# Tying the gain scalings and the splits of the K, Q and gate weights behind the first matmul of the projection before

## The chip, the cores and the metric

The kernel runs on one core of one Trainium2 chip. The metric is the device time of one execution in microseconds; lower is better. Before the change it is 2731.74 us (the median of three runs, 2731.46 to 2737.39).

## What is computed

A two-layer encoder trunk over 2048 frames of width 1024, in float32. Layer A is a gated MLP, layer B is chunked attention with a relative-position bias whose keys and values come from the output of layer A. Cut to what matters here:

```
h  = rms_norm(x, a_norm_g);  u, v, z = split(h @ w_in, 3)
x  = x + (gelu(u) * (W_s LayerNorm(gelu(v)) + b) * silu(z)) @ w_out      # layer A
k, v = split(rms_norm(x, kv_norm_g) @ w_kv, 2)                           # shared K and V
q, z = split(rms_norm(x, b_norm_g) @ w_qz, 2)
o  = softmax(q k^T / 8 + bias, own chunk and the 8 chunks before) v      # 16 heads of 64
x  = x + (o * silu(z)) @ w_b_out
out = rms_norm(x, final_norm_g)
```

## The kernel before

**Arithmetic.** Every float32 matrix product is made of three matmuls on operands that are split into a high and a low part (`mm3`, lines 112 to 115: high by high, high by low, low by high). A split is one cast on ScalarE (ACT) that makes the high part and one subtraction on VectorE (DVE) that makes the low part.

**Stages.** Layer A comes first, then the V projection for the four sequence tiles of 512 frames, then stage B: the attention and the output product. This stage starts with the first projection matmul at 1549.0 us and reaches the end of the program.

**Stage B.** The outer loop runs over the four tiles t, the inner one over the eight pairs p of heads. A pair needs three projections: Q (c = 1), K (c = 0) and the gate z (c = 2). Each is one call of `one` (lines 1214 to 1223): it fetches a 128 x 1024 block of weights with `weights` (lines 189 to 200), takes one PSUM bank, and makes 8 x 3 = 24 matmuls into it. So there are 96 projections, 24 to each tile. While a pair's scores, softmax, transposes and value products run, the projections of the next pair, and a part of the output product of the tile before, are mixed in between, some matmuls at a time (`ahead`, lines 1581 to 1600).

**A projection's weights.** In the first tile (t = 0) `weights` loads the block from the input (line 196), GpSimd (POOL) multiplies it by the norm's gain (`scaled`, lines 170 to 173), a DMA stores the scaled block for later tiles (line 198), and `split_in` (lines 185 to 187) casts it into `wh` on ACT and subtracts it into `wl` on DVE. In the later tiles the scaled block is loaded (line 194) and only split. The raw block has four buffers in the first tile, which are shared with the activations' tiles, and two of its own later. `wh` and `wl` come from a pool of eight buffers (`w_tile`), which the output product's weights use too: four projections can be prepared ahead, where nothing else holds the pool.

**What sets the order.** The program is written out flat. The framework decides at build time, by its own estimate of times, in which order each engine's instructions are queued; at run time each engine takes its queue in order, with semaphores where there is a dependency of data or buffers. All DMAs of this kernel are issued from the SP queue, in order too. An extra edge between two instructions, without a semaphore (`add_manual_dep` with the class NoSync), tells this ordering that one instruction comes after another. Layer A already uses such edges in a helper:

```python
def paced(ins):
    if "evict" in last:
        behind(ins, last["evict"])
```

It ties, for example, the POOL product of `merge_u` (line 756) behind the latest DVE eviction.

**The end of the V stage.** The V projection of the last tile takes its left operands from splits `Shv` and `Slv` (lines 269 and 270); its evictions are DVE subtractions (line 1136), ACT casts (line 1135) and POOL additions (line 1159).

Of the kernel before, what the change touches and what calls it, by code (L numbers as in the profile page):

```python
# [13 lines left out]
ALU = mybir.AluOpType  # L14
# [3 lines left out]
P = 128  # L18
S = 2048
D = 1024  # L20
KD = D // P
# [12 lines left out]
def trunk_kernel(  # L34
# [19 lines left out]
    nc = tc.nc  # L54
# [32 lines left out]
    kg = cst.tile([P, KD, 1], F32, name="kg")  # L87
    bg = cst.tile([P, KD, 1], F32, name="bg")
# [21 lines left out]
    mm, tpose = nc.tensor.matmul, nc.tensor.transpose  # L110

    def mm3(ps, lh, ll, rh, rl, first, last):
        mm(ps, lh, rh, start=first, stop=False)  # L113
        mm(ps, lh, rl, start=False, stop=False)  # L114
        mm(ps, ll, rh, start=False, stop=last)  # L115

    xT = {}
    xf = {}
# [41 lines left out]
    def reload(t):  # L160
        th, tl = x_tiles(t)
        for b in range(TB):
# [4 lines left out]
            nc.scalar.copy(oh, x3)  # L167
            tv(tl[:, :, b * P : (b + 1) * P], x3, oh.bitcast(F32), op=sub)

    def scaled(raw, gain):  # L170
        k = gain.shape[1]
        r3 = raw[:].rearrange("p (k c) -> p k c", k=k)
        nc.gpsimd.tensor_tensor(r3, r3, gain.broadcast_to([P, k, 1024 // k]), op=ALU.mult)

    def w_tile(name):
        return sh.tile([P, 1024], F32R, tag="T", name=name, bufs=8)
# [3 lines left out]
    def raw_w(t, name):  # L180
        if t:
            return raws[0].tile([P, 1024], F32, tag="wr", name=name, bufs=2)
        return sh.tile([P, 1024], F32, tag="raw", name=name, bufs=4)

    def split_in(raw, wh, wl):
        nc.scalar.copy(wh[:], raw[:])  # L186
        tv(wl[:], raw[:], wh[:].bitcast(F32), op=sub)  # L187

    def weights(t, p, c):
        name = f"b{t}_{p}_{c}"  # L190
        raw = raw_w(t, f"raw_{name}")
        w = w_tile(f"wh_{name}"), w_tile(f"wl_{name}")
        if t:
            nc.sync.dma_start(raw[:], wk3[p][c][:])
        else:
            nc.sync.dma_start(raw[:], w_kqz[p, :, c, :])
            scaled(raw, (bg if c else kg)[:, :, :])
            nc.sync.dma_start(wk3[p][c][:], raw[:])
        split_in(raw, *w)
        return w  # L200

    def o_right(t):
# [19 lines left out]
    def v_early(q, ph):  # L222
        if q == 0:
            tag = "hh" if ph == 1 else "hl"
            big = sh.tile([P, 4, 1024], F32R, tag=tag, name=f"vw_{ph}")
            for i in range(2):
                vw[ph, i] = (big[:, 2 * i, :], big[:, 2 * i + 1, :])
        raw = sh.tile([P, 1024], F32, tag="raw", name=f"rv_{ph}_{q}", bufs=4)
        nc.sync.dma_start(raw[:], vwf[ph, q][:])
        return lambda: split_in(raw, *vw[ph, q])  # L230
# [3 lines left out]
    def strassen(name, right, left, evict, look):  # L234

        todo = [(ph, jp) for ph in PHS for jp in range(2)]
        rts, views = {}, {}

        def weigh(n):
            for ph in PHS[:n]:  # L240
                if ph not in rts:
                    rts[ph] = right(ph)

        def ready(i):
            if i < len(todo):
                views[i] = left(*todo[i])

        weigh(1)
        ready(0)
        for i, (ph, jp) in enumerate(todo):  # L250
            ps = pmm.tile([P, 512], F32, tag="mm", name=f"{name}_{ph}_{jp}")
            vs = views.pop(i)
            for k in range(4):
                hi, lo = rts[ph][k // 2]
                c = slice((k % 2) * 512, (k % 2) * 512 + 512)
                mm3(ps[:], *vs[k], hi[:, c], lo[:, c], k == 0, k == 3)
                if k == 1:
                    weigh(i // 2 + (2 if jp else 1 + look))
                    ready(i + 1)
                if k < 3:  # L260
                    yield
            evict(ph, jp, ps[:])
            yield
# [46 lines left out]
    with ExitStack() as actx:  # L310
# [169 lines left out]
        def product(ps, s, t):  # L480

            nk = len(s)
            for k in range(nk):
                hi, lo = t[k // 2]
                c = slice((k % 2) * 512, (k % 2) * 512 + 512)
                mm3(ps[:], s[k][0], s[k][1], hi[:, c], lo[:, c], k == 0, k == nk - 1)
# [248 lines left out]
        def mix(n, r, q, part):  # L735
            vh, vl = mixp[n, r, q]
            ws = wsp[n]
            if part == 0:
                mt[n, r, q] = up[0].tile([P, 2, 512], F32, tag="m", name=f"m{n}_{r}_{q}", bufs=4)
            m = mt[n, r, q]  # L740
            px = up[1].tile([P, 2, 2, P], F32, tag="mx", name=f"mx{n}_{r}_{q}_{part}", bufs=2)
            hs = [2 * part, 2 * part + 1]
            cs = [slice(h * P, h * P + P) for h in hs]
            for i, (h, c) in enumerate(zip(hs, cs)):
                mm3(
                    px[:, i], ws[:, 0, h, :], ws[:, 1, h, :], vh[:, :, c], vl[:, :, c], True, True
                )
            for i, (h, c) in enumerate(zip(hs, cs)):
                hh = (n - 2) * 4 + h
                nc.scalar.activation(  # L750
                    m[:, :, c], px[:, i], AF.Identity, scale=0.5, bias=bsh[:, hh : hh + 1]
                )
# [50 lines left out]
        start = {}  # L803
# [387 lines left out]
    with ExitStack() as bctx:  # L1191
# [22 lines left out]
        def one(t, p, c):  # L1214
            wh, wl = weights(t, p, c)
            acc = pmm.tile([P, T], F32, tag="mm", name=f"pj{t}_{p}_{c}")
            for k in range(KD):
                hh, hl = xT[t][k]
                sl = slice(k * P, (k + 1) * P)
                mm3(acc[:], wh[:, sl], wl[:, sl], hh, hl, k == 0, k == KD - 1)  # L1220
                if k < KD - 1:
                    yield None
            yield acc

        def project(t, p):
            for acc in one(t, p, 1):
                yield
            for hd in range(2):
                qh = sb.tile([P, T], F32R, tag="Q", name=f"Qh{t}_{p}_{hd}", bufs=8)
                ql = sb.tile([P, T], F32R, tag="Q", name=f"Ql{t}_{p}_{hd}", bufs=8)  # L1230
                r, r2 = halves(hd)
                nc.scalar.mul(qh[r, :], acc[r, :], 0.125)
                nc.vector.scalar_tensor_tensor(
                    ql[r, :], acc[r, :], 0.125, qh[r, :].bitcast(F32),
                    op0=ALU.mult, op1=ALU.subtract,
                )
                for x_ in (qh, ql):
                    nc.sync.dma_start(x_[r2, :].bitcast(F32), x_[r, :].bitcast(F32))
                qt[t, p, hd] = (qh, ql)
            for acc in one(t, p, 0):  # L1240
                yield
            for hd in range(2):
                r, r2 = halves(hd)
                kx = sb.tile([P, 2 * T], F32R, tag="K", name=f"K{t}_{p}_{hd}", bufs=4)
                nc.scalar.copy(kx[r, T:], acc[r, :])
                nc.vector.tensor_tensor(
                    kx[r2, T:], acc[r, :], kx[r, T:].bitcast(F32), op=ALU.subtract
                )
                if t + 1 < NT:
                    nc.sync.dma_start(khd[t][p][hd], kx[:, T:].bitcast(F32))  # L1250
                if t > 0:
                    nc.sync.dma_start(kx[:, :T].bitcast(F32), khd[t - 1][p][hd])
                kt[t, p, hd] = kx
# [7 lines left out]
        def gate(t, p):  # L1261
            for acc in one(t, p, 2):
                yield
            z = sb.tile([P, T], F32, tag="Z", name=f"Z{t}_{p}", bufs=2)
            nc.scalar.activation(z[:], acc[:], AF.Tanh, scale=0.5)
            nc.vector.scalar_tensor_tensor(
                z[:], z[:], 1.0, acc[:], op0=ALU.add, op1=ALU.mult
            )
            zt[t, p] = z
# [311 lines left out]
        def ahead(t, p):  # L1581

            if p + 1 < NPAIR:
                yield from project(t, p + 1)
                values(t, p + 1)
                if p == 0:
                    yield from gate(t, 0)
                yield from gate(t, p + 1)
                if t:
                    yield from some(outs[t - 1], SHARE[t][p])  # L1590
            else:
                if t + 1 < NT:
                    reload(t + 1)
                if t:
                    yield from some(outs[t - 1], 4)
                if t + 1 < NT:
                    yield from project(t + 1, 0)
                    values(t + 1, 0)
                if t:
                    yield from some(outs[t - 1], 8)  # L1600
# [9 lines left out]
        first = ahead(0, 0)  # L1610
# [103 lines left out]
```

## Time and profile before

| | before |
|---|---|
| median of 3 runs | 2731.74 us |
| profiled execution, its own time | 2731.49 us |
| profiled execution, span of its instructions | 2729.7 us |
| mean granted TensorE clock | 0.987 |
| TensorE (PE) busy | 2629.2 us, 96% |
| VectorE (DVE) busy | 1970.0 us, 72% |
| ScalarE (ACT) busy | 1327.0 us, 49% |
| GpSimd (POOL) busy | 907.7 us, 33% |

The profile is of one execution, which took 2731.49 us, 1.79 us of them outside the span and 0.25 us under the median. PE's bar is high throughout, so the time that can be won or lost is in the single stretches where it waits, and in the stretches in which its clock is granted at half. In a row of the timeline stand the start, the length, the engine, the source line, the operation with its output and inputs, how many were merged, and in brackets the idle time before it with what ended it. A row of the waits has the waiter and the one waited for, then the total in us, the number of times, and the longest.

### The profile page before, as it was taken

What the parts mean: (1) busy time and instruction counts of PE and PEld (TensorE: products, weight loads), DVE (VectorE), ACT (ScalarE), POOL (GpSimd) and SP (SyncE); (2) the same over time, 40 slices, a digit from 0 to 9 for tenths busy, and PEclk for the clock granted to TensorE, in tenths of its full rate; (3) what the DMA queues carried; (4) which work ended last, traced back from release to release, by engine and by line L of the source; (5) the groups of instructions that cost most, each with busy time, mean ns of one, the idle gap of its engine ahead of it and who ended that gap; (6) DMA issues with size and microseconds to landing.
All of it is one profiled execution on the core that took longest, in us unless ns stands there. A gap on an engine that the chain in (4) does not pass through costs nothing. (4 is left out here: it accounts for less than half of the span.)

```text
span 2729.7 us, 38869 instructions
## 1 busy us (share of the span) xinstructions
PE 2629.2 (96%) x13216; PEld 2199.6 (81%) x13216; DVE 1970.0 (72%) x3097; ACT 1327.0 (49%) x2360; POOL 907.7 (33%) x906
## 2 busy tenths in 40 slices
PE   8999999999999999999989899899999999999997
PEld 7788888888888888888867677788887888788875
DVE  5655676676666668667677777777778778877787
ACT  5422242433434345332455455656656566656553
POOL 3512226142351314114234444323232223323243
PEclk9999999999999999999989999999999999999999
DMA  8898999989989879678668778766777667866677
GB/s 299 309 332 335 348 353 327 332 299 352 333 301 310 286 269 345 224 244 318 236 221 283 250 249 256 253 207 196 231 247 256 204 220 229 272 197 193 187 227 248
DMA packets 274774, 735.57 MB, mean 269 GB/s; under 512 B 29584, under 2 KB 61328, under 8 KB 274576
## 3 DMA queue, kind: packets, MB, share of 16 engines
q1 hardware_dynamic: 274576, 733.09, 78.3%
q8 instruction: 105, 1.72, 0.2%
q14 instruction: 93, 0.76, 0.1%
HBM read 540.56 MB, written 181.93 MB: 265 GB/s over the span
## 5 line engine op out<-in xcount | busy, mean ns | idle before, releaser
L113 PE MATMUL P<-T,S 128*128 128x512 f32 x1248 | 495.0, 397 | 2.1 <-ACT S L360 2.1
L115 PE MATMUL P<-T,S 128*128 128x512 f32 x1248 | 489.4, 392 | 0.0
L114 PE MATMUL P<-T,S 128*128 128x512 f32 x1248 | 488.1, 391 | 1.1 <-DVE T L363 1.1
L1321 POOL TENSOR_SCALAR pr<-pr,sl 128x640 f32<-128x640 f32 (+4 forms) x256 | 201.9, 789 | 548.1 <-DVE sl L1320 494.6
L113 PE MATMUL pj<-hh_b,wh_b 128*128 128x512 f32 x768 | 316.2, 412 | 6.0 <-ACT wh_b L186 4.2
L1317 ACT ACTIVATE pr<-pr,nm 128x640 f32<-128x640 f32 (+4 forms) x256 | 195.5, 764 | 229.1 <-DVE nm L1310 224.0
L114 PE MATMUL pj<-hl_b,wh_b 128*128 128x512 f32 x768 | 306.2, 399 | 0.0
L115 PE MATMUL pj<-hh_b,wl_b 128*128 128x512 f32 x768 | 305.6, 398 | 0.0
L115 PEld LDWEIGHTS P<-T,S 128*128 128x128 f32 x1248 | 234.8, 188 | 50.1
L113 PEld LDWEIGHTS P<-T,S 128*128 128x128 f32 x1248 | 235.2, 189 | 46.8 <-ACT S L360 2.3
L114 PEld LDWEIGHTS P<-T,S 128*128 128x128 f32 x1248 | 235.2, 188 | 46.6 <-DVE T L363 1.3
L1345 DVE TENSOR_TENSOR pt<-tp,pt 128x640 fp32r<-128x640 f32 (+4 forms) x256 | 188.7, 737 | 74.6 <-ACT pt L1344 72.5
L1310 DVE CUSTOM_DVE_ANT_0 pr<-s,bias 128x640 f32<-128x640 f32 (+4 forms) x256 | 188.1, 735 | 26.0 <-PE s L1302 20.7
L1341 PE MATMUL tp<-ident,pr 128*128 128x128 f32 x1120 | 167.0, 275 | 19.5 <-DVE pt L1345 16.9
L1341 PEld LDWEIGHTS tp<-ident,pr 128*128 128x128 f32 x1120 | 134.8, 141 | 63.2 <-issue 21.4
L1344 ACT CAST pt<-tp 128x640 fp32r<-128x640 f32 (+4 forms) x256 | 158.7, 620 | 52.7 <-PE tp L1341 49.9
L115 PEld LDWEIGHTS pj<-hh_b,wl_b 128*128 128x128 f32 x768 | 146.6, 191 | 32.7
L113 PEld LDWEIGHTS pj<-hh_b,wh_b 128*128 128x128 f32 x768 | 147.5, 192 | 25.7 <-ACT wh_b L186 5.8
L114 PEld LDWEIGHTS pj<-hl_b,wh_b 128*128 128x128 f32 x768 | 147.3, 192 | 16.9
L187 DVE TENSOR_TENSOR wl_b<-raw_b,wh_b 128x1024 fp32r<-128x1024 f32 x96 | 126.6, 1320 | 29.1 <-ACT wh_b L186 28.0
L1369 PE MATMUL pv<-pt,V 128*128 128x256 f32 x960 | 142.4, 288 | 0.9 <-ACT pt L1344 0.9
L1369 PEld LDWEIGHTS pv<-pt,V 128*128 128x128 f32 x960 | 127.0, 193 | 3.1 <-ACT pt L1344 1.8
(291 smaller groups left out, 5952.6 us busy)
## 6 DMA issues: line engine op xcount, KB each, us to landing
S<-hsd SPq DMA_DIRECT2D x288, 512.0 KB, 5.5
rw<-in_w_a SPq DMA_DIRECT2D x108, 512.0 KB, 6.4
A<-ytd SPq DMA_DIRECT2D x72, 512.0 KB, 5.8
raw_b<-wk SPq DMA_DIRECT2D x72, 512.0 KB, 3.9
hsd<-S SPq DMA_DIRECT2D x56, 512.0 KB, 4.4
V<-vhd SPq DMA_DIRECT2D x56, 512.0 KB, 4.7
wh_bo<-ows SPq DMA_DIRECT2D x50, 512.0 KB, 4.4
wl_bo<-ows SPq DMA_DIRECT2D x50, 512.0 KB, 5.6
```

The costliest lines, as they stand in the source:

```text
L113: mm(ps, lh, rh, start=first, stop=False)
L114: mm(ps, lh, rl, start=False, stop=False)
L115: mm(ps, ll, rh, start=False, stop=last)
L187: tv(wl[:], raw[:], wh[:].bitcast(F32), op=sub)
L1310: nc.vector.tensor_tensor_reduce(out=pr[:, c0:].rearrange("p (a b) -> p a b", a=nseg), in0=ps[:, :nseg, :w], in1=bias[:, c0:].rearrange("p ...
L1317: nc.scalar.activation(pr[:, c0:], pr[:, c0:], AF.Exp, scale=-1.0, bias=nm[:], accum_out=sl[:])
L1321: nc.gpsimd.tensor_scalar(pr[:, c0:], pr[:, c0:], sl[:], 1.0, op0=ALU.mult, op1=ALU.mult)
L1341: tpose(tp[:, b, :], pr[:, b * P : (b + 1) * P], ident[:])
L1344: nc.scalar.copy(oh, tp[:, b0:5, :])
L1345: nc.vector.tensor_tensor(pt[:, 1, b0 + qq : 5 + qq, cs], tp[:, b0:5, :], oh.bitcast(F32), op=ALU.subtract)
L1369: mm(po[:, 0, :], keys(i), pt[:, j, i, :], start=(t == 0 and j == 0 and i == blocks[0]), stop=(j == 1 and i == blocks[-1]),)
```

## The change

In the first tile, POOL's scaling of a projection's weights gets an edge without a semaphore behind the first matmul of the projection that was written just before it. In the later tiles, where nothing is scaled, the ACT cast that makes the high part gets this edge. The first projection of all has none before it and stays free. To have a name to tie to, `mm3`, `scaled` and `split_in` return an instruction, and `one` notes the first matmul of each projection. No arithmetic, transfer, buffer or loop changes.

```diff
     def mm3(ps, lh, ll, rh, rl, first, last):
-        mm(ps, lh, rh, start=first, stop=False)
+        first = mm(ps, lh, rh, start=first, stop=False)
         mm(ps, lh, rl, start=False, stop=False)
         mm(ps, ll, rh, start=False, stop=last)
+        return first
...
+    pace = []
+
+    def paced_by_pj(ins):
+        if pace:
+            tc.add_manual_dep(
+                ins.ins, pace[-1],
+                mybir.DependencyInfo(mybir.DependencyClass.NoSync, mybir.DependencyReason.DATA),
+                reason="order",
+            )
...
     def split_in(raw, wh, wl):
-        nc.scalar.copy(wh[:], raw[:])
+        hi = nc.scalar.copy(wh[:], raw[:])
         tv(wl[:], raw[:], wh[:].bitcast(F32), op=sub)
+        return hi
...
             nc.sync.dma_start(raw[:], w_kqz[p, :, c, :])
-            scaled(raw, (bg if c else kg)[:, :, :])
+            paced_by_pj(scaled(raw, (bg if c else kg)[:, :, :]))
             nc.sync.dma_start(wk3[p][c][:], raw[:])
-        split_in(raw, *w)
+        hi = split_in(raw, *w)
+        if t:
+            paced_by_pj(hi)
         return w
...
-                mm3(acc[:], wh[:, sl], wl[:, sl], hh, hl, k == 0, k == KD - 1)
+                ins = mm3(acc[:], wh[:, sl], wl[:, sl], hh, hl, k == 0, k == KD - 1)
+                if k == 0:
+                    pace.append(ins.ins.name)
```

More of the change, by code (lines that the diff above doesn't have):

```diff
@@ L172, in scaled @@
         r3 = raw[:].rearrange("p (k c) -> p k c", k=k)
-        nc.gpsimd.tensor_tensor(r3, r3, gain.broadcast_to([P, k, 1024 // k]), op=ALU.mult)
+        return nc.gpsimd.tensor_tensor(
+            r3, r3, gain.broadcast_to([P, k, 1024 // k]), op=ALU.mult
+        )
     def w_tile(name):
```

## The prediction

> **What bounds the kernel now.** I read the page first, then the waits of the matmul engine stage by stage, then the timeline of each engine around the longest waits.
>
> ```profile
> span 2729.7 us, 38869 instructions
> PE 2629.2 (96%) x13216; PEld 2199.6 (81%) x13216; DVE 1970.0 (72%) x3097; ACT 1327.0 (49%) x2360; POOL 907.7 (33%) x906
> PEclk9999999999999999999989999999999999999999
> ```
>
> PE is busy for all but 100 us, so no edit of other engines' work can bring more than this and what PE loses at a lower clock. The edit touches the end of the V stage and stage B; the waits of PE from 1500 to 1800 us (the first tile with its way in and out) and one row of those from 1800 us on:
>
> ```profile
> PE tp L1341 <- DVE pt L1345: 9.7, 11, 2.3
> PE vp L115 <- DVE Slv L270: 5.6, 1, 5.6
> PE s L1302 <- DMA Qh<-Qh: 4.4, 1, 4.4
> PE s L1302 <- DVE K L1246: 3.8, 1, 3.8
> PE s L1302 <- DVE nm L1310: 2.6, 4, 1.7
> PE pj L113 <- ACT wh_b L186: 4.2, 3, 2.0
> ```
>
> The last row is the only one in which PE waits for a projection's weights, and it is of the later tiles: in the first tile the weights are never late. The two longest single waits there, 5.6 and 4.4 us, are the ones to look at. The first, from the timelines of POOL, DVE and PE:
>
> ```profile
> 1518.24 2.07 POOL L173 TENSOR_TENSOR raw_b<-raw_b,bg 128x1024 f32<-128x1024 f32 x1 [5.96 <-DMA raw_b<-in_w_kqz]
> 1520.31 2.04 POOL L173 TENSOR_TENSOR raw_b<-raw_b,kg 128x1024 f32<-128x1024 f32 x1
> 1522.31 2.07 POOL L173 TENSOR_TENSOR raw_b<-raw_b,bg 128x1024 f32<-128x1024 f32 x1
> ...
> 1534.34 1.61 POOL L1159 TENSOR_TENSOR vu<-vu,vu 128x512 f32<-128x512 f32 x1 [2.24 <-ACT wh_b L186]
> ```
>
> ```profile
> 1518.47 4.15 DVE L1136 TENSOR_TENSOR v<-vc,v 128x256 fp32r<-128x256 f32 x2
> 1522.55 2.38 DVE L270 TENSOR_TENSOR Slv<-xo_b,Shv 128x512 fp32r<-128x512 f32 x1
> ...
> 1526.65 0.75 DVE L1136 TENSOR_TENSOR v<-vc,v 128x256 fp32r<-128x256 f32 x2
> 1527.33 0.68 DVE L270 TENSOR_TENSOR Slv<-xo_b,Shv 128x512 fp32r<-128x512 f32 x1
> ```
>
> ```profile
> 1518.74 0.39 PE L114 MATMUL vp<-vwl,Shv 128*128 128x512 f32 x1
> 1518.96 0.39 PE L113 MATMUL vp<-vwh,Shv 128*128 128x512 f32 x1
> 1524.98 0.80 PE L115 MATMUL vp<-vwh,Slv 128*128 128x512 f32 x1 [5.63 <-DVE Slv L270]
> ```
>
> Three scalings of projections that first run at 1549 us and later go back to back from 1518.24 to 1524.38. In just that time a pair of DVE subtractions takes 4.15 us instead of 0.75, and the next one 2.38 instead of 0.68; each ends as a scaling ends. PE stands still for 5.63 us, and then its clock is halved. These are windows with PE's granted clock in the last column but two, and the wait that stands before the second:
>
> ```profile
> 1524.10:1530.90 6.80, 5.92 (x14) 4.72 (x15) 5.14 (x9) 1.85 (x4) 0.69 (x2) 0.50 0.75 273
> 1563.00:1567.30 4.30, 0.00 (x0) 0.01 (x1) 0.69 (x1) 1.80 (x2) 3.10 (x4) 0.74 1.04 289
> 1636.80:1640.20 3.40, 3.40 (x12) 2.91 (x11) 1.34 (x4) 1.85 (x5) 1.09 (x5) 0.50 0.94 355
> 1708.40:1711.80 3.40, 3.40 (x13) 2.82 (x12) 2.14 (x6) 1.95 (x6) 3.20 (x3) 0.51 0.91 353
> ```
>
> ```profile
> 1634.96 0.33 PE L1302 MATMUL s<-K,Qh 128*128 128x128 f32 x1 [1.74 <-DVE nm L1310]
> ```
>
> After 5.63 us of idleness PE runs at 0.50 for 6.8 us; after 1.74 and after 3.8 us, for 3.4 us. Half speed for 6.8 us costs 3.4 us, for 3.4 us it costs 1.7.
>
> **What the edge does.** The kernel has edges of this kind already. For the POOL product that layer A ties behind a DVE eviction, the view of its line says:
>
> ```profile
> L756 POOL TENSOR_TENSOR c<-c,m x32: 1296/1746/2340, 383.4 to 934.0; 128x512 f32<-128x512 f32 x32
> ...
>   ACT c L770: 2.6, 2
> ```
>
> Its only wait is for the ACT result that it reads, none for the DVE eviction. So I take the edge as a place in the queue and not as a wait: nothing is held at run time, but the scaling stands behind whatever POOL has queued by then, and with it move its store, the cast, the subtraction, and the load that takes over its buffer, on POOL, SP, ACT and DVE.
>
> **Part 1, the end of the V stage.** The first scaling is not tied and stays; the second and third go behind the V stage's last POOL work (1534.34). The blocked pair then ends when the first scaling does, at 1520.31, plus its own 0.75; the split `Slv` follows with 0.68: 1521.74 instead of 1522.55 + 2.38 = 1524.93. Gain **3.2 us**. PE's idle time falls to 2.4 us, between the 1.74 and 3.8 that drew one 3.4 us window; so one window of two is left. Gain **1.7 us** (bounds 0 and 3.4).
>
> **Part 2, the opening of stage B.**
>
> ```profile
> 1556.82 1.51 SPq L196 DMA_DIRECT2D raw_b<-in_w_kqz  x2
> 1558.43 0.42 SPq L1198 DMA_DIRECT2D gf<-in_fin_g  x1
> ...
> 1559.42 0.67 SPq L1238 DMA_DIRECT2D Qh<-Qh  x1
> ```
>
> ```profile
> 1567.32 0.45 PE L1302 MATMUL s<-K,Qh 128*128 128x128 f32 x1 [4.35 <-DMA Qh<-Qh]
> ```
>
> The first scores wait for a small copy of Q that was issued behind two weight loads; the DMA engines are full (1.04 of their time, 289 GB/s, in the window above). A load of 128 x 1024 x 4 bytes is 0.524 MB, 1.8 us at this rate. Its buffer comes free when the weights four projections before are split. With the splits of projections 2 and 3 later, I expect one of the two loads to fall behind the copy: gain **1.8 us** (bounds 0 and 3.6).
>
> **Part 3, the rest of the first tile.** What the preparation costs, and how often it is needed:
>
> ```profile
> L173 POOL TENSOR_TENSOR raw_b<-raw_b,bg x16: 1894/1900/2076, 1518.2 to 1730.0; 128x1024 f32<-128x1024 f32 x16
> L186 ACT CAST wh_b<-raw_b x96: 1028/1050/1065, 1531.3 to 2614.9; 128x1024 fp32r<-128x1024 f32 x96
> L187 DVE TENSOR_TENSOR wl_b<-raw_b,wh_b x96: 1203/1224/2352, 1532.4 to 2616.4; 128x1024 fp32r<-128x1024 f32 x96
> ...
> L113 PE MATMUL pj<-hh_b,wh_b x192: 388/396/736, 1549.0 to 1766.8; 128*128 128x512 f32 x192
> ```
>
> Scaling, cast and subtraction take 1.90 + 1.05 + 1.22 = 4.2 us bare. The last row is of the window from 1545 to 1768 us: 192 matmuls in eights are 24 projections in 217.8 us, one each 9.1 us. Counting that line's rows in eights gives each projection's first matmul; for the last K projection of the tile the scaling starts here, and the first matmuls of the projection before it and of its own are
>
> ```profile
> 1721.51 2.97 POOL L173 TENSOR_TENSOR raw_b<-raw_b,kg 128x1024 f32<-128x1024 f32 x1
> ```
>
> ```profile
> 1741.32 0.40 PE L113 MATMUL pj<-hh_b,wh_b 128*128 128x512 f32 x1
> ...
> 1749.65 0.40 PE L113 MATMUL pj<-hh_b,wh_b 128*128 128x512 f32 x1
> ```
>
> Now it is 19.8 us ahead of the matmul it will be tied to. Tied, the chain of 4.2 us has on average 9.1 us: 4.9 are left for standing in the queues of POOL, ACT and DVE. In the opening, projections run back to back: 24 matmuls at the 0.225 us spacing of the V rows above are 5.4 us, which leaves 1.2. Cover is thinner but there: **0** (bounds below; a gain is possible where a 1.9 us scaling no longer stands before a score's work, as much as the 9.7 us of waits for `pt`). Behind a scaling on POOL stand the softmax products (L1321), behind a cast on ACT the exponentials; the number of these operations per projection is as before.
>
> The Trainium skill (SBUF — State Buffer, section Who interferes with whom) speaks against the new place: a DVE operation with two SBUF inputs is shut out by a GpSimd one that reads SBUF for as long as that runs, and the weights' subtraction has two such inputs. The trace agrees with its 2352 ns at most against 1224. By this rule the 23 tied scalings could stretch 23 subtractions by 1.13 us each, 26 us of DVE, which counts for the time only where the lead is gone.
>
> **Part 4, the later tiles.** Here only the cast is tied, and mostly it sits at this place already, as its buffers come free no earlier:
>
> ```profile
> 1868.54 1.06 ACT L186 CAST wh_b<-raw_b 128x1024 fp32r<-128x1024 f32 x1
> ```
>
> ```profile
> 1868.81 0.39 PE L113 MATMUL pj<-hh_b,wh_b 128*128 128x512 f32 x1
> ```
>
> The cast starts 0.27 us ahead of the matmul that it is to follow, and its own projection comes 9 us later. Cover: 9.1 us against 1.05 + 1.22. I put **0** (bounds: -4.2 if the three late casts of the second table go, +4.2 if as many come).
>
> **Sum.** 3.2 + 1.7 + 1.8 = 6.7 us off the profiled execution's 2731.49: **2724.8 us**, 0.25% under it, and as good as that under the median of 2731.74. A measurement of this kernel tells 0.2%, 5.5 us, from no change.
>
> **Rivals.** *The lead was needed.* Where the queues hold a chain for more than the 4.9 us (1.2 in the opening), PE waits, at 1.4 us a time (4.2 us in three waits). If 8 of the 23 tied projections of the first tile do so, that is 11.2 us, and if half of these waits draw a half-clock window of 3.4 us, 6.8 more: 2724.8 + 18 = 2742.8 us. For it: the 9.7 and 2.6 us of waits in this tile show that DVE's queue already runs late at times. Against it: order alone holds nothing back at run time. *A place in the queue changes little.* POOL is idle two thirds of the time, so the moved scalings may run nearly as early, or new waits pay back the rest: the 3.2 us of part 1 alone would give 2728.3, with one or two new waits 2731. *No half-clock window is left.* This is a clock that needs more idleness than 2.4 us before it halves: 1.7 us more, 2723.1. The rows speak against it, as 1.74 us were enough. The Trainium skill (TensorE: Matmul & The Clock Gate, section Part 1) has such a rule: the half rate after at least one idle window of about 3.4 us; by it this rival's 2723.1 would hold, and the trace does not agree.
>
> **How the numbers follow.** Forecast 0.40, within 2717 to 2731 by the bounds of parts 1 to 4; no half-clock window left 0.05; little change 0.22; lead needed 0.33. So faster by over 0.2% has 0.45, within 0.2% 0.22, slower 0.33. For 8 in 10 the range reaches from 2715 us, the forecast with part 3 giving back most of its waits for `pt`, to 2750 us, the lead rival with about five more waits.
>
> **What would show it.** Right: one scaling instead of three before 1525 us, the wait for `Slv` at about 2.4 us, one half-clock window there, the first `Qh` copy nearer, no row of PE waiting for `wh_b` or `wl_b` before 1768 us, and scalings within 2 or 3 us of the first matmul they are tied to. Wrong: rows of `pj` waiting for `wh_b` or `wl_b` in the first tile, or longer waits of `tp` and `s` at the changes of tiles.

## The result, and the profile after

The changed kernel takes **2723.72 us** (median of 15 runs, 2719.49 to 2731.61), the kernel before 2730.66 us (median of 15 runs beside them, 2726.17 to 2737.95). The ratio is **0.9976** (95% interval 0.9967 to 0.9985): 6.6 us less, with 4.1 to 9.0 us in the interval. The forecast was 6.7 us less.

The two profiled executions hide this: that of after happened to be the longest of its 15 runs, with a mean granted clock of 0.986 (its 15 runs have 0.986 to 0.991), and that of before lies near its median. So the spans differ by 1.1 us only, and single stretches have to be compared. From the page of after:

```profile
span 2728.6 us, 38857 instructions
PE 2630.1 (96%) x13216; PEld 2199.9 (81%) x13216; DVE 1961.0 (72%) x3097; ACT 1324.8 (49%) x2360; POOL 909.8 (33%) x906
```

**End of the V stage.** The timelines of POOL, DVE and PE of after, with the rows that answer to the blocked pair and to the 5.63 us of before (line 1152 is the old 1136, 286 the old 270, 184 the old 173):

```profile
1523.21 2.07 POOL L184 TENSOR_TENSOR raw_b<-raw_b,bg 128x1024 f32<-128x1024 f32 x1 [5.95 <-DMA raw_b<-in_w_kqz]
1530.32 1.61 POOL L1175 TENSOR_TENSOR vu<-vu,vu 128x512 f32<-128x512 f32 x1 [5.04 <-DVE vu L1174]
1533.75 1.61 POOL L1175 TENSOR_TENSOR vu<-vu,vu 128x512 f32<-128x512 f32 x1 [1.83 <-DVE vu L1174]
1535.32 1.90 POOL L184 TENSOR_TENSOR raw_b<-raw_b,kg 128x1024 f32<-128x1024 f32 x1
1537.18 2.08 POOL L184 TENSOR_TENSOR raw_b<-raw_b,bg 128x1024 f32<-128x1024 f32 x1
```

```profile
1523.44 2.46 DVE L1152 TENSOR_TENSOR v<-vc,v 128x256 fp32r<-128x256 f32 x2
1525.82 0.68 DVE L286 TENSOR_TENSOR Slv<-xo_b,Shv 128x512 fp32r<-128x512 f32 x1
```

```profile
1526.55 0.50 PE L115 MATMUL vp<-vwh,Slv 128*128 128x512 f32 x1 [2.20 <-DVE Slv L286]
```

One scaling is left, to 1525.28; the pair of subtractions ends 0.62 us after it and takes 2.46 us instead of 4.15, the split after it its bare 0.68, and PE waits 2.20 us instead of 5.63. The other two scalings stand behind the last POOL sums. This is what the prediction described.

**Opening of B.** The SP queue of after has one weight load ahead of the first Q copy where there were two:

```profile
1553.11 0.34 SPq L210 DMA_DIRECT2D raw_b<-in_w_kqz  x1
1553.55 0.41 SPq L1214 DMA_DIRECT2D gf<-in_fin_g  x1
1554.01 0.42 SPq L1297 DMA_DIRECT2D bias<-reld  x1
1554.53 1.33 SPq L1256 DMA_DIRECT2D Qh<-Qh  x1
```

```profile
1567.47 0.39 PE L1320 MATMUL s<-K,Qh 128*128 128x256 f32 x1 [2.19 <-DVE nm L1328]
```

The copy is issued 6.8 us after the first `pj` matmul (1547.76) instead of 10.4 us, and the wait of 4.35 us for it is gone. In its place a score waits 2.19 us for `nm` of an earlier score.

**First tile.** Here the waits of PE changed hands. From the waits of PE between 1545 and 1778 us, after:

```profile
PE pv L1387 <- ACT pt L1362: 10.2, 4, 4.2
PE s L1320 <- DVE nm L1328: 3.5, 3, 2.2
PE tp L1359 <- DVE pt L1363: 3.5, 7, 0.9
PE tp L1359 <- POOL pr L1339: 3.2, 1, 3.2
PE pj L113 <- ACT wh_b L199: 1.9, 1, 1.9
```

The 9.7 us of `tp` for `pt` fell to 3.5, but `pv` now waits 10.2 us for `pt`, which it did not before, and one `pj` waits for its weights. How `pt` comes to be late is seen in the timelines of ACT, DVE and PE around the longest of these waits:

```profile
1662.22 0.60 ACT L1250 ACTIVATE Qh<-pj 64x512 fp32r<-64x512 f32 x1
1667.86 1.04 ACT L199 CAST wh_b<-raw_b 128x1024 fp32r<-128x1024 f32 x1 [5.04 <-POOL raw_b L184]
1668.92 0.59 ACT L1250 ACTIVATE Qh<-pj 64x512 fp32r<-64x512 f32 x1
1669.54 0.51 ACT L1335 ACTIVATE pr<-pr,nm 128x256 f32<-128x256 f32 x1
1669.95 0.19 ACT L1335 ACTIVATION_READ_ACCUMULATOR pr<-pr,nm 128x1 f32 x1
1670.17 0.59 ACT L1362 CAST pt<-tp 128x512 fp32r<-128x512 f32 x1
```

```profile
1668.93 1.22 DVE L200 TENSOR_TENSOR wl_b<-raw_b,wh_b 128x1024 fp32r<-128x1024 f32 x1 [4.66 <-ACT wh_b L199]
```

```profile
1670.81 0.39 PE L1387 MATMUL pv<-pt,V 128*128 128x256 f32 x1 [4.24 <-ACT pt L1362]
```

ACT's queue has come to the weights' cast; the scaling before it runs from 1665.93 to 1667.83 on POOL, and ACT stands for 5.04 us. Behind the cast stand `Qh`, an exponential and the cast of `pt`, all of which have nothing to do with these weights, and DVE stands the same way at the subtraction. PE runs out of work and waits 4.24 us for that `pt`. PE does not wait for the weights; it waits for what stands behind them. Each of the waits of PE of over 1.9 us after 1600 us in this tile (2.34, 3.17, 4.24, 1.92 and 3.48 us) follows such a standing of ACT at a weights' cast, of 1.58 to 5.04 us; only that of 1.92 us is a wait for the weights themselves.

### The profile page after: what moved, and what is told of

The parts are those of the page before. It is cut to its first block, busy times and chain, and to the rows that moved or that the text cites. A ratio compares the mean times of both kernels' runs of the same rounds, so it can differ in the third digit from the quotient of the medians.

```text
span 2728.6 us, 38857 instructions
## 1 busy us (share of the span) xinstructions
PE 2630.1 (96%) x13216; PEld 2199.9 (81%) x13216; DVE 1961.0 (72%) x3097; ACT 1324.8 (49%) x2360; POOL 909.8 (33%) x906
## 5 line engine op out<-in xcount | busy, mean ns | idle before, releaser
L1387 PEld LDWEIGHTS pv<-pt,V 128*128 128x128 f32 x960 | 127.5, 193 | 14.9 <-ACT pt L1362 13.6
```

What stands on the lines that cost most here:

```text
L1387: mm(po[:, 0, :], keys(i), pt[:, j, i, :], start=(t == 0 and j == 0 and i == blocks[0]), stop=(j == 1 and i == blocks[-1]),)
```

## The experiments

Each experiment's ratio is to the kernel before, run beside it on the same chip. Stretches are counted from rows of PE: the V stage from the first `vp` to the first `pj` matmul, the tiles from one tile's first `pj` matmul to the next one's. A stretch of a single profile is not exact: the first tile of e_later, with no scaling tied there, as before, is 4.3 us shorter than that of before, at a mean clock of 0.99 instead of 0.96.

| kernel | ratio (95% interval) | wait for `Slv`, us | V stage, us | first tile, us | second tile, us |
|---|---|---|---|---|---|
| before | 1 | 5.63 | 199.0 | 224.4 | 288.6 |
| after | 0.9976 (0.9967 to 0.9985) | 2.20 | 195.6 | 229.7 | 284.4 |
| e_again | 0.9976 (0.9963 to 0.9988) | 2.04 | 193.1 | 226.9 | 285.0 |
| e_vend | 0.9982 (0.9969 to 0.9995) | 1.91 | 196.1 | 226.5 | 288.2 |
| e_tile0 | 0.9988 (0.9977 to 1.0000) | 1.90 | 194.6 | 228.2 | 286.4 |
| e_later | 0.9987 (0.9975 to 0.9999) | 5.47 | 198.7 | 220.1 | 288.1 |
| e_two | 0.9987 (0.9973 to 1.0002) | 3.60 | 198.2 | 226.8 | 289.8 |
| e_zero | 0.9980 (0.9968 to 0.9992) | 0.53 | 191.7 | 228.5 | 285.2 |
| e_vend_later | 0.9969 (0.9957 to 0.9982) | 1.91 | 194.3 | 222.7 | 285.3 |
| e_cast3 | 0.9910 (0.9893 to 0.9927) | 1.90 | 193.4 | 208.0 | 286.4 |
| e_cast_only | 0.9944 (0.9926 to 0.9961) | 5.30 | 198.9 | 211.1 | 286.3 |
| e_cast5 | 0.9958 (0.9944 to 0.9973) | 2.07 | 195.5 | 217.6 | 285.7 |
| e_cast_all3 | 0.9931 (0.9917 to 0.9946) | 1.90 | 195.9 | 209.9 | 287.4 |
| e_cast3_zero | 0.9912 (0.9896 to 0.9929) | 0.29 | 192.4 | 208.5 | 285.5 |

**e_again: the kernel after, once more.** No edit.

> The kernel after, unchanged, for a second profile. Theory A (three parts: the end of the V stage gains about 6 us, the ties of the rest of the first tile lose about 5, the ties of the later tiles gain about 4): from the cast hh_b nearest before the last V splits to the first pj matmul 28 to 29 us (before 34.9), the first tile from its first pj matmul to the next tile's about 229 us (before 224.4), the second tile about 284.5 (before 288.6); time about 2724. Theory B (only the end of the V stage counts; the other two are chance of one slow execution): first tile 224 to 226 us, second tile about 288, the same time.

The same ratio. The second profile repeats the waits of the first, the longest again as `pv` for `pt` (4.37 us), so they belong to the order of the queues and not to one execution. First tile 226.9 us, second 285.0: nearer to theory A.

**e_vend: the ties of the second and third projection's scalings alone.**

```diff
-            paced_by_pj(scaled(raw, (bg if c else kg)[:, :, :]))
+            ins = scaled(raw, (bg if c else kg)[:, :, :])
+            if len(pace) <= 2:
+                paced_by_pj(ins)
...
-        if t:
-            paced_by_pj(hi)
```

> Only the scalings of the second and third projection are tied, behind the first and the second projection's first matmul; all other preparation is left to the order of before. Theory A: the 6 us of the V stage without the first tile's loss and without the later gain: 2724 to 2725 us, first tile 224 to 225, second 288 to 289. Theory B: all that the change brings, 2723 to 2724 us. A time of 2729 or more would say that the end of the V stage isn't what brings the gain.

0.18% or 4.9 us: two of the 23 ties of the first tile bring most of what the whole change brings. The first tile at 226.5 us is longer than theory A had it; it has waits of 3.36, 2.13, 2.36 and 3.50 us of `tp` for `pt`, each just behind a weights' cast that stood 2.4 to 4.5 us for its scaling.

**e_tile0: all ties of the first tile, none later.**

```diff
-        if t:
-            paced_by_pj(hi)
```

> The ties of all 23 scalings of the first tile, none of the later casts. Theory A: the gain of 6 us at the end of the V stage is nearly eaten by the first tile's new waits (pv for pt, tp for pr): 2729 to 2730 us, first tile about 229 us. Theory B: 2723 to 2725 us, first tile 224 to 226.

0.12% or 3.3 us, between the two theories, with an interval that reaches to no change, and not better than two ties alone: the other 21 ties show no gain. The first tile is that of theory A.

**e_later: the ties of the later casts alone.**

```diff
-            paced_by_pj(scaled(raw, (bg if c else kg)[:, :, :]))
+            scaled(raw, (bg if c else kg)[:, :, :])
```

> Only the casts of the later tiles are tied; the first tile is that of before. Theory A: 4 us less than before, 2726 to 2727 us, second tile 284 to 285 us, no 2.4 us gap of PE near 2030 us. Theory B: within 1 us of before.

0.13% or 3.5 us by the times, as theory A had it. But its profile does not show where: the second tile is 288.1 us and the 2.4 us gap is still there (at 2028 us). So the size fits and the place named does not.

**e_two: one tie alone, that of the third projection.**

```diff
-            paced_by_pj(scaled(raw, (bg if c else kg)[:, :, :]))
+            ins = scaled(raw, (bg if c else kg)[:, :, :])
+            if len(pace) == 2:
+                paced_by_pj(ins)
...
-        if t:
-            paced_by_pj(hi)
```

> One of the 23 ties alone: the scaling of the third projection, so that two scalings instead of three (before) or one (after) stand at the end of the V stage. If each scaling there shuts DVE out for its own 1.9 to 2.1 us, PE's wait for Slv is about 3.9 us, between 5.5 and 2.1; the other theory (the casts and subtractions of the weights that moved with the scalings took DVE's time) leaves it at 5 or more, or takes it to 2. The whole time is between the two kernels, 0.999 of before.

**e_zero: after, with the first scaling out of the V stage too.** The edit is in the V stage's eviction, at its POOL sum.

```diff
-                    tg(y_, y_, x_, op=add)
+                    vl = tg(y_, y_, x_, op=add)
+                    if t + 1 == NT:
+                        pace.append(vl.ins.name)
```

> The kernel after, with the first projection's scaling tied too, behind the last POOL sum of the V stage: no scaling is left where DVE splits S. If the rest of PE's wait for Slv (2.0 to 2.2 us) is the one scaling that stayed, it falls under 0.6 us and the kernel gains 1.5 to 3 us on after (ratio to before 0.9965 to 0.997). If the wait is the splits of hh and hl in front, it stays at 2 us. If the first projection's weights come too late, PE waits for wh_b or wl_b at the first pj matmul, up to 2 us, and nothing is gained.

PE's row at the first `Slv` in e_two, and DVE's and PE's rows of e_zero:

```profile
1526.88 0.79 PE L115 MATMUL vp<-vwh,Slv 128*128 128x512 f32 x1 [3.60 <-DVE Slv L286]
```

```profile
1519.68 0.75 DVE L1152 TENSOR_TENSOR v<-vc,v 128x256 fp32r<-128x256 f32 x2
```

```profile
1521.09 0.50 PE L115 MATMUL vp<-vwh,Slv 128*128 128x512 f32 x1 [0.53 <-DVE Slv L286]
```

For e_two this is near the 3.9 us expected. With three, two, one and no scaling in that place PE waits 5.63, 3.60, 1.9 to 2.2 and 0.53 us: 1.4 to 2.0 us for each scaling (they take 1.9 to 2.7 us there), and without any the pair takes its bare 0.75 us. That the scalings shut DVE out there is shown. The V stage follows (199.0 us in before, 198.2 in e_two, 194.8 on average over the eight kernels with one scaling, 191.7 and 192.4 without any). The time of e_zero does not: 0.9980 against 0.9976, though a gain of 1.5 us is inside the intervals. PE waits 0.25 + 0.53 us for the second projection's weights there, and none for the first's. The ratio of e_two, 0.9987, is as expected, but not clear of no change.

**e_cast3: after, with the casts of the first tile tied later.** The cast goes behind the fourth of the eight groups of the preceding projection's matmuls; the scaling stays behind the first.

```diff
-    def paced_by_pj(ins):
+    pace3 = []
+
+    def paced_by_pj(ins, pace=pace):
...
-        if t:
-            paced_by_pj(hi)
+        paced_by_pj(hi, pace if t else pace3)
...
                 if k == 0:
                     pace.append(ins.ins.name)
+                if k == 3:
+                    pace3.append(ins.ins.name)
```

> The kernel after, with the casts of the first tile tied too, behind the fourth of eight groups of the preceding projection's matmuls. Theory of the blocked queue: in the first tile of after, ACT stands at a cast until POOL's scaling ends (27 to 29 us in all), and the exponentials and casts of pt behind it are late, so that PE waits for pt and pr. Then ACT's standing for raw_b falls under 15 us, the waits of pv for pt of 2 to 4 us go, and the kernel is 3 to 5 us faster than after (ratio to before 0.996). Theory of the lost lead: the later cast makes pj wait for wh_b and wl_b, 1.4 us a time in several of 23 projections, and the kernel is slower than after by 3 us or more (ratio 0.999 or higher).

The largest gain of all, on four runs: 0.90% under before, 0.66% or 18 us under after, several times the 3 to 5 us expected. The groups of instructions between 1545 and 1778 us, the weights' cast in before, after and e_cast3 (busy time and mean, then ACT's idle time in front of it and what ended it):

```profile
L186 ACT CAST wh_b<-raw_b 128x1024 fp32r<-128x1024 f32 x24 | 25.2, 1049 | 25.8 <-POOL raw_b L173 18.9 <-PE pj L114 3.2 <-DMA raw_b<-wk 2.0
```

```profile
L199 ACT CAST wh_b<-raw_b 128x1024 fp32r<-128x1024 f32 x24 | 25.2, 1050 | 28.7 <-POOL raw_b L184 20.0 <-DMA Qh<-Qh 4.4 <-DMA V<-vhd 4.0
```

```profile
L201 ACT CAST wh_b<-raw_b 128x1024 fp32r<-128x1024 f32 x27 | 28.3, 1047 | 8.5 <-POOL raw_b L186 5.5 <-DMA V<-vhd 2.8
```

ACT stands 8.5 us at these casts instead of 28.7 (the stretch holds three casts of the next tile in e_cast3). From PE's waits in the same stretch of e_cast3:

```profile
PE tp L1362 <- DVE pt L1366: 3.7, 7, 1.4
PE s L1323 <- DVE nm L1331: 2.6, 3, 1.7
PE pj L113 <- ACT wh_b L201: 1.9, 1, 1.9
...
PE pv L1390 <- ACT pt L1365: 0.9, 1, 0.9
```

The waits of `pv` for `pt` are gone but for 0.9 us, and the wait for weights is still one of 1.9 us. With the waits the half-clock windows go; the first tile of after and of e_cast3 as windows (PE's granted clock in the last column but two):

```profile
1547.76:1777.47 229.71, 202.16 (x1000) 164.00 (x998) 151.21 (x354) 128.76 (x289) 97.04 (x147) 0.95 0.78 252
```

```profile
1546.26:1754.25 207.99, 193.92 (x1001) 157.98 (x999) 152.16 (x354) 128.75 (x289) 97.07 (x147) 0.99 0.86 279
```

The 21.7 us between them are 13.5 us less in which PE was not busy (27.6 and 14.1 us) and 8.2 us by which PE was busy for a shorter time with the same matmuls, at a mean clock of 0.99 instead of 0.95. The expectation had counted only waits.

**e_vend_later: two ties at the V stage and the later casts.**

```diff
-            paced_by_pj(scaled(raw, (bg if c else kg)[:, :, :]))
+            ins = scaled(raw, (bg if c else kg)[:, :, :])
+            if len(pace) <= 2:
+                paced_by_pj(ins)
```

> The first two ties of the first tile (e_vend) and the casts of the later tiles (e_later), without the other 21 ties of the first tile. If the parts add up, 0.9982 and 0.9987 make 0.9969, 8 us less than before; if the ties of the rest of the first tile bring something of their own, it is slower than after (0.9976); if the later casts count only together with them, 0.998.

0.9969, as the parts add up. Nothing says that the other 21 ties of the first tile help (after has 0.9976, with an overlapping interval).

**e_cast_only: before, with the later casts of the first tile alone.** As e_cast3, with no scaling and no later cast tied.

```diff
-            paced_by_pj(scaled(raw, (bg if c else kg)[:, :, :]))
+            scaled(raw, (bg if c else kg)[:, :, :])
...
-        paced_by_pj(hi, pace if t else pace3)
+        if not t:
+            paced_by_pj(hi, pace3)
```

> The kernel before with one thing added: the casts of the first tile tied behind the fourth group of the preceding projection's matmuls; no scaling and no later cast is tied. If the blocked queue of ACT is what costs in the first tile whatever the place of the scalings, most of the gain of e_cast3 is had without the change: first tile 208 to 213 us, time 2713 to 2718 (ratio 0.993 to 0.9945), with the wait for Slv at the end of the V stage still 5.5 us. If the tied scalings are needed for it (POOL waits for loads in the order of before: 35 us of idleness at raw_b), the first tile stays at 218 us or more and the ratio at 0.997 or more.

0.9944: 15 us less than before without any part of the change, and the first tile at 211.1 us, although PE still waits 5.30 us for `Slv`: the first theory, in each of its figures. Between 1545 and 1778 us ACT now stands 2.2 us at the casts, where before has 25.8:

```profile
L201 ACT CAST wh_b<-raw_b 128x1024 fp32r<-128x1024 f32 x28 | 29.3, 1049 | 2.2 <-POOL raw_b L186 1.5 <-DMA raw_b<-wk 0.4
```

So the blocked queue was there before the change, and the change left it.

**e_cast5: the cast behind the sixth group.** As e_cast3, with

```diff
-                if k == 3:
+                if k == 5:
```

> As e_cast3, with the casts behind the sixth of eight groups instead of the fourth, some 2.3 us later at 9.1 us a projection. Here the lead must run out: the cast and the subtraction take 1.05 + 1.22 us and the two groups left about 2.3 us. Theory of the lost lead, now at its proper place: waits of pj for wh_b or wl_b in the first tile come back, 0.5 to 1.5 us in many of the projections, 3 to 10 us slower than e_cast3. If ACT and DVE reach cast and subtraction at once, it is the same as e_cast3 within 2 us.

0.9958, by the ratios 13 us slower than e_cast3, with an uncertainty of some 6 us; 3 to 10 were expected. Its waits from 1545 to 1746 us have the row that was looked for:

```profile
PE pj L115 <- DVE wl_b L202: 4.4, 7, 1.2
```

In e_cast3 this is one wait of 0.4 us. The cover has an end, and it lies between the fourth and the sixth group.

**e_cast_all3: the later tiles' casts moved to the fourth group too.**

```diff
-        paced_by_pj(hi, pace if t else pace3)
+        paced_by_pj(hi, pace3)
```

> As e_cast3, with the casts of the later tiles too moved from behind the first group to behind the fourth. There the weights come scaled from memory and ACT stands at a cast for 1 to 2 us a tile only, so nothing is to be had: within 2 us of e_cast3; if a load is what a cast waits for, up to 2 us faster; if the lead is too short there, waits of pj for wh_b and 2 to 4 us slower.

0.9931 against 0.9910: nothing gained, and about 6 us lost by the midpoints, but the intervals overlap. What would cost them I have not found; its second tile is 1.0 us longer than that of e_cast3.

**e_cast3_zero: both together.** The edits of e_cast3 and e_zero.

> e_cast3 and e_zero together: no scaling at the end of the V stage and later casts in the first tile. If the 1.5 us that e_zero took off PE's wait for Slv count, 1 to 3 us faster than e_cast3 (ratio 0.9900 to 0.9905); if not, the same.

0.9912, the same as e_cast3 within the intervals. PE's wait for `Slv` is 0.29 us, but, as in e_zero, the whole time does not show it. The fastest version found is e_cast3 (2709.21 us, median) or this one (2705.79 us, measured at another time); the runs do not tell them apart.

## Why the prediction was right in the sum, and where it was not

**The total** was forecast at 6.7 us less and came at 6.6, 0.24%: just beyond the 0.2% that the prediction called distinguishable, with the lower end of the interval (0.15%) inside it. The rival *little change* is thus not far off, and would have been right without the later tiles. The terms were less good than their sum. By the ratios, e_vend stands for parts 1 and 2, e_tile0 against e_vend and after against e_vend_later for part 3, and after against e_tile0 and e_vend_later against e_vend for part 4:

| part | predicted, us | by the ratios, us |
|---|---|---|
| 1 and 2: V stage and opening | -6.7 | -4.9 |
| 3: rest of the first tile | 0 | +1.6 and +1.9 |
| 4: later tiles | 0 | -3.3 and -3.5 |

By these midpoints parts 3 and 4, both put at 0, and a shortfall of 1.8 us in the first two cancel; that the sum came within 0.1 us is luck. A difference of two such ratios is uncertain by some 4 to 5 us, and the two figures of a part are not independent of those of the other, as each pair adds up to the same difference between after and e_vend. So the sign of part 3 is not shown. That of part 4 has e_later beside it (-3.5 us, -6.8 to -0.3 in its interval).

**The edge.** It holds nothing at run time, as predicted: the second and third scaling run at 1535.32 and 1537.18, 12 and 16 us *ahead* of the matmuls that they are tied to. The others start from 4 us before to 10 us after theirs, not all within 2 or 3.

**Part 1.** The wait was predicted at 2.4 us and is 1.90 to 2.20; its mechanism was shown by the row of three, two, one and no scalings. The clock term was put at one half-clock window left of two. In the profile of after there was none, in that of e_vend there was one:

```profile
1523.00:1530.00 7.00, 4.80 (x21) 3.63 (x20) 7.00 (x11) 3.18 (x7) 2.07 (x1) 1.00 0.78 280
```

```profile
1523.70:1527.10 3.40, 3.40 (x10) 2.66 (x9) 2.40 (x5) 1.38 (x4) 0.00 (x0) 0.51 0.96 338
```

```profile
1523.08 0.50 PE L115 MATMUL vp<-vwh,Slv 128*128 128x512 f32 x1 [1.91 <-DVE Slv L286]
```

Of the eight profiles with one scaling, four have such a window there and four none; so the 1.7 us is 2.6 on average, and the rival "no half-clock window is left" is half right. The term took the length of the wait for what decides; it is where the wait falls, as the last section shows. The V stage as a whole gained 4.1 us (198.9 on average over before, e_later and e_cast_only, to 194.8) of the 4.9 forecast. Wait and windows alone would make 6.1 us; where the rest went in this stage is not shown.

**Part 2.** Right in its steps: one load fell behind the copy, the wait of 4.35 us went and another of 2.19 us stands in its place, 2.2 us less where 1.8 were forecast. What the term left out is the clock, which part 1 had priced: after the wait of 4.35 us PE ran at half for 6.8 us in before, after that of 2.19 us for 3.4 us in after (the window at 1569.10 in the last section), a further gain of 1.7 us.

```profile
1565.10:1571.90 6.80, 4.58 (x12) 3.74 (x13) 0.30 (x2) 0.49 (x2) 1.06 (x3) 0.50 0.85 266
```

**Part 3** is the step that failed, though not in its number. It said "behind a cast on ACT the exponentials; the number of these operations per projection is as before", and looked for a lost lead in rows of `pj` waiting for `wh_b` or `wl_b`. What matters is not how many stand behind the cast but how long the cast itself stands, and this was in the trace of before: 18.9 us of ACT waiting for POOL. The waits of `tp` for `pt`, which I counted as a possible gain, were the outer end of that chain: in e_cast_only they fall from 9.7 us to 2.4. The change reshuffled it (25.8 us of standing, then 28.7) and gave back about what it took; e_cast_only and e_cast3 show that it is worth 15 to 18 us. The *lead was needed* rival looked at the wrong row for the same reason. In the first tile there was one wait for `wh_b`, of 1.9 and 2.3 us in the two profiles of the changed kernel, where that rival had eight. Nor did the weights' subtractions stretch beside the scalings as the prediction priced it, at up to 26 us of DVE. Between 1545 and 1778 us they take 1286 ns on average both in before and in after, and 1414 in e_cast_only, which is the faster kernel, so they are not what the first tile pays for:

```profile
L187 DVE TENSOR_TENSOR wl_b<-raw_b,wh_b 128x1024 fp32r<-128x1024 f32 x26 | 33.4, 1286 | 18.8 <-ACT wh_b L186 18.8
```

```profile
L200 DVE TENSOR_TENSOR wl_b<-raw_b,wh_b 128x1024 fp32r<-128x1024 f32 x24 | 30.9, 1286 | 29.6 <-ACT wh_b L199 29.4
```

```profile
L202 DVE TENSOR_TENSOR wl_b<-raw_b,wh_b 128x1024 fp32r<-128x1024 f32 x28 | 39.5, 1414 | 4.8 <-ACT wh_b L201 4.3 <-DMA Ql<-Ql 0.4
```

**Part 4** was put at 0 with bounds of 4.2 us, and is about -3.4. In the order of before, DVE stands 1.93 us for a load of `y`, with `pt` behind it, and PE waits:

```profile
2027.91 0.75 DVE L1521 SCALAR_TENSOR_TENSOR y<-y,rr_f,gf 128x512 f32<-128x512 f32 x1 [1.93 <-DMA y<-x2d]
2028.58 0.82 DVE L1345 TENSOR_TENSOR pt<-tp,pt 128x640 fp32r<-128x640 f32 x1
```

```profile
2029.54 0.88 PE L1341 MATMUL tp<-ident,pr 128*128 128x128 f32 x3 [2.42 <-DVE pt L1345]
```

With both kinds of ties that wait is 0.7 us or less (after, e_again, e_vend_later); with the later casts alone it stays (e_later). So the gain in the second tile seems to come of a new interleaving (e_cast_only, with no later tie, has 286.3 us there too) and was not in the moved cast, where I looked; the three waits for `wh_b` that I set as its bound are still there (4.8 us after, 4.2 before). For e_later's gain no place is shown, and that stays open.

## What to carry to other kernels

When an engine's queue is taken in order, a preparation that is put too early costs what stands behind it: look in the trace for an instruction that waits long for its own operand (here ACT's cast, 18.9 us) and for the waits of *other* tiles that end just after it, and price those. Of a chain of operations on several engines, place each link by itself: the first link (the scaling) where it disturbs nobody, the next one only when the first will have ended, with its end still ahead of the use; here the middle of the preceding projection was worth 18 us beside the whole change's 6.6, and two groups later some 13 of them were lost again. A short wait also costs what it does to the clock, 8 us beside 13.5 us here.

## What was not expected of the hardware

**Half-clock windows lie on a grid.** Three of them as windows of the profile of after:

```profile
1569.10:1572.50 3.40, 3.40 (x11) 2.55 (x10) 3.09 (x8) 2.42 (x6) 1.36 (x4) 0.50 0.84 312
1705.60:1712.40 6.80, 5.39 (x15) 4.62 (x16) 3.14 (x10) 3.49 (x9) 2.92 (x9) 0.50 0.91 321
1671.50:1674.90 3.40, 3.35 (x12) 2.60 (x11) 1.64 (x6) 1.24 (x4) 1.72 (x4) 0.50 0.81 266
```

Their starts are 102.4 and 34.1 us apart, 30 and 10 times 3.41 us, and they last one or two times that. In the fourteen profiles all 189 half-clock stretches start on such a grid of 3.41 us, which lies differently against the program in each.

What decides is how long PE is idle within one window of the grid, not how long a single wait is. Counted over the fourteen profiles from 1000 us on, after a window at full clock: all 131 with 2.0 us of idleness or more were followed by half the clock, 21 of the 37 with 1.7 to 2.0 us, and 2 of the 6641 with less. This explains why a wait of 1.9 to 2.2 us at one place of the program drew a half-clock window in four profiles and none in four: in the four with one, 1.9 to 2.3 us of idleness fell into one window of the grid, in the four without the wait lay across the border of two, with at most 1.81 us in one. First the two windows over which the wait of after lies (the busy time of PE is the first column behind the length), then the one ahead of the half-clock window of e_vend:

```profile
1521.33:1524.74 3.41, 3.02 (x14) 2.14 (x12) 3.41 (x4) 2.99 (x7) 1.53 (x1) 1.00 0.95 328
1524.74:1528.15 3.41, 1.60 (x7) 1.34 (x8) 3.41 (x6) 1.02 (x3) 0.54 (x1) 1.00 0.63 229
```

```profile
1520.24:1523.65 3.41, 1.07 (x4) 0.68 (x5) 3.41 (x5) 0.90 (x2) 1.56 (x1) 1.00 0.43 172
```

The clock also goes with most of the spread of 12 us over the 15 runs of after: granted clocks of 0.986 to 0.991, and 0.005 of 2722 us are 13.6 us. The Trainium skill (TensorE: Matmul & The Clock Gate, Part 1) describes the window as free-running, 3413 ns long, and the trace agrees with that. Its "after ≥1 idle window (~3.4µs)" the trace does not bear out: in e_vend the window ahead of the half clock had 2.34 us of idleness, 1.91 of them in one wait.

**DVE and POOL.** The Trainium skill (SBUF — State Buffer, Who interferes with whom) has a DVE operation with two SBUF inputs shut out by a GpSimd one that reads SBUF; the trace agrees: the pair `v<-vc,v` took 4.15 us beside the scalings of before, 2.46 beside the one of after, and 0.75 beside none (e_zero).
